# The adaLN product-sums of later stages issued from the scan's z units, and decayed x dt split one step later

## The chip, the cores and the metric

The kernel runs on one core of one Trainium2 chip. The metric is the device time of one execution in microseconds; the kernel before was run three times. Five engines work side by side: TensorE (PE; its weight loads are shown as PEld), VectorE (DVE), ScalarE (ACT), GpSimd (POOL) and SyncE (SP), which here issues nearly all DMAs. Each engine takes its instructions in the order in which the built program holds them; what they need from each other is settled by semaphores.

## What is computed

One block of a model with 512 tokens and a width of 1024, in float32. A vector c gives, through one 1024 x 6144 matrix, six vectors of 1024 that shift, scale and gate the two sub-layers:

```python
mod = (jax.nn.silu(c) @ w_ada[i] + b_ada[i])[:, None, :]
shift_m, scale_m, gate_m, shift_f, scale_f, gate_f = jnp.split(mod, N_MOD, axis=-1)
h = rmsnorm(x, norm_mix_w[i]) * (1.0 + scale_m) + shift_m
x = x + gate_m * hybrid_mixer(h, ...)
h = rmsnorm(x, norm_mlp_w[i]) * (1.0 + scale_f) + shift_f
x = x + gate_f * (jnp.square(jax.nn.relu(h @ w_up[i])) @ w_down[i])
```

The mixer projects h to z, x, B, C, dt, a pooling input and two gates. x, B and C pass a causal convolution of width 4 and a silu. Then a scan over 4 chunks of 128 tokens runs in 4 groups of 8 heads:

```python
scores = jnp.einsum('bclgn,bcsgn->bgcls', cc, bc)
mmat = scores[:, :, None] * segsum_decay(a_cs)
y_diag = jnp.einsum('bghcls,bcsghp->bclghp', mmat, x)
decay_states = jnp.exp(a_cs[..., -1:] - a_cs)
states = jnp.einsum('bcsgn,bghcs,bcsghp->bcghpn', bc, decay_states, x)
```

Here x is already multiplied by dt = softplus(dt_raw + bias). The scan's output is multiplied by silu(z) and normed by group; branch projections, sigmoid gates and an output projection follow, then the MLP.

## The kernel before

Every large product is made of *units*: 128 rows of an output, contracted over 1024. `unit` loads 512 KB of weights into a RAW slot (`load_unit`, L139; four slots d0 to d3), ACT rounds them to a high part (L144), DVE subtracts to get the low part (L145), both into one pair of the HL buffers, and PE makes 8 x 3 matmuls of 128x128 by 512 (L154 to L156: high x high, high x low, low x high). PSUM banks for units come from PU (three of them at this stage), those for the scan from PS.

A *product-sum* is `ada(j)` (L166 to L171): SP loads 512 KB of the transposed adaLN matrix into a RAW slot, the same four slots that the weights use, and one DVE instruction (L170) multiplies it by silu(c) and adds it up into one of 48 columns of `mod`; a second small one reads the accumulator. Sums 0 to 15 (shift and scale of the mixer) are made at the start, through other buffers. Sums 16 to 47 are needed from the output projection on: 16 to 23 gate the mixer, 24 to 39 shift and scale the MLP's input, 40 to 47 gate the MLP.

The stages follow each other so: the opening up to 53 us, where PE is fed h; a high-priority part (L329 to L364) that makes dt by a softplus chain of small DVE instructions (L340 to L354), sums it along tokens on PE (L356), copies the result (L357, which frees the PSUM bank), transposes it (L360) and writes it to DRAM (`cs_d`, `ecs_d`); the convolutions of group 0 (L381 to L383) and its four z units z0 to z3 (`u_z`); then `run`, which drives `ssd_group` for groups 0 to 3 and puts other units between its steps as fillers. z0 is given the PSUM bank that the softplus chain uses, so it cannot begin before L357.

In `ssd_group`, `prepare(c)` loads the decay rows of chunk c (L476), makes the decay factors (L478 to L480), masks (POOL, L481), exponentiates (L485), multiplies by the scores (L486), transposes x (L489), multiplies it by dt (L491), lets POOL multiply that by the decay (L497), and splits the product into a high part (ACT, L124) and a low part (DVE, L125). The main loop first prepares chunk c + 1 and then takes chunk c: it makes the state product with `mm3` (PE, L154 to L156 with two s tiles) and the output (L535).

The order on each engine is set when the program is built: a scheduler goes through the program by priority and by its own estimate of when each instruction could run. A moved call therefore moves other instructions too. Only the opening is written out by hand.

Of the kernel before, what the change touches and what calls it, by code (L numbers as in the profile page):

```python
# [61 lines left out]
def block_kernel(tc, xp, crow, arow, par, adaT, wstart, wz, wx, wpool_in, wgate, wpw, wbs, wbp, wout, wup, wdn, out):  # L62
# [3 lines left out]
    with (  # L66
# [13 lines left out]
        S = slots("s", NSLOT)  # L80
# [38 lines left out]
        done = [None]  # L119

        def split(src):

            hi, lo = S.get(F32R), S.get(F32R)
            act.copy(hi, src)  # L124
            done[0] = dve.tensor_tensor(lo, src, hi.bitcast(F32), ALU.subtract)  # L125
            return hi, lo
# [39 lines left out]
        def ada(j, at=RAW):  # L166

            r = at.get()
            sp.dma_start(r, adaT[j])
            dve.tensor_tensor_reduce(r, r, cbc, 1.0, col("b_ada", j), ALU.mult, ALU.add, mod[:, j:j + 1])  # L170
            at.put(r)  # L171

        def column_sums(ps, sqs, c0, c1, opened=False):

# [42 lines left out]
        with tc.manual_schedule():  # L217
# [74 lines left out]
            for k in range(8):  # L292
                hi, lo = S.get(F32R), S.get(F32R)
                h.append((hi, lo))
                t = S.get()
# [73 lines left out]
        for u in range(1, 7):  # L369
            t = S.get()  # L370
# [49 lines left out]
        def u_z(g, i):  # L420
            def f():
                if "sz" not in G[g]:
                    G[g]["sz"] = SZ.get()
                ps = unit(wz[4 * g + i], h)
                with tc.issue_after(act.activation(G[g]["sz"][:, i, :], ps, AF.Silu).ins):
                    silus()
                PU.put(ps)
            return f

        acc = [None] * 8  # L430

        def bs(g, jp):

            def f():
                w = load_unit(wbs[4 * g + jp])
                for jj in range(2):
                    j = 2 * jp + jj
                    ps = PU.get()
                    for k in range(4):
                        mm3(ps, w[4 * jj + k], G[g]["y"][k], k == 0, k == 3)  # L440
                    if g == 0:
                        acc[j] = S.get()
                        act.copy(acc[j], ps)
                    else:
                        dve.tensor_tensor(acc[j], acc[j], ps, ALU.add)
                    PU.put(ps)
                if jp == 3:
                    free(G[g]["y"])
            return f

        def ssd_group(g):
# [20 lines left out]
            def prepare(c):  # L472

                cc = slice(c * P, (c + 1) * P)
                m = MT.get()
                sp.dma_start(m, cs_d[heads, cc].partition_broadcast(P))  # L476
                if c < 3:
                    act.activation(cdg[:, c, :], m[:, :, P - 1], AF.Exp)  # L478
                    dve.tensor_tensor(decg[:, c, :], m[:, :, P - 1], ncs[:, c, heads], ALU.add)
                    act.activation(decg[:, c, :], decg[:, c, :], AF.Exp)  # L480
                pool.affine_select(  # L481
                    m, m, pattern=[[0, HG], [1, P]], compare_op=ALU.is_ge, fill=-1e30, base=0,
                    channel_multiplier=-1)
                for i in range(HG):
                    act.activation(m[:, i, :], m[:, i, :], AF.Exp, bias=ncs[:, c, g * HG + i:g * HG + i + 1])  # L485
                dve.tensor_tensor(m, m, sc[:, cc].unsqueeze(1).broadcast_to([P, HG, P]), ALU.mult)  # L486
                ps = PS.get()
                for i in range(4):
                    pe.transpose(ps[:, i * P:(i + 1) * P], xs[:, i, cc], ident)  # L489
                xdt = S.get()  # L490
                dve.tensor_tensor(  # L491
                    v3(xdt), v3(ps), dtk[:, c, heads].unsqueeze(2).broadcast_to([P, HG, 64]), ALU.mult)
                PS.put(ps)
                xd = None
                if c < 3:
                    t = S.get()
                    pool.tensor_tensor(  # L497
                        v3(t), v3(xdt), decg[:, c, :].unsqueeze(2).broadcast_to([P, HG, 64]), ALU.mult)
                    xd = split(t)
                    S.put(t)  # L500
                return m, xdt, xd

            ready = [prepare(0)]
            yield
            for c in range(NC):
                cc = slice(c * P, (c + 1) * P)
                if c < NC - 1:
                    ready.append(prepare(c + 1))
                    yield
                m, xdt, xd = ready.pop(0)  # L510
                yo = None
                if c > 0:
                    yo = PS.get()
# [112 lines left out]
        def pool_mix(gp):  # L626
            def f():
                w = load_unit(wpw[gp])
                for gi in (2 * gp, 2 * gp + 1):
                    for d in range(2):  # L630
                        ps = PU.get()
                        for k in range(2):
                            mm3(ps, w[((gi % 2) * 2 + d) * 2 + k], held[gi, k], k == 0, k == 1)
                        t = S.get()
                        act.activation(t, ps, AF.Copy, scale=col("pscale", 2 * gi + d))
                        PU.put(ps)
                        pout.append(split(t))
                        S.put(t)
                    free([held[gi, 0], held[gi, 1]])
            return f  # L640
# [45 lines left out]
        for j in range(8):  # L686
            gp = F.get()
            ps = unit(wgate[8 + j], h)
            behind(act.activation(gp, ps, AF.Sigmoid))
            PU.put(ps)  # L690
            merged.append(gp)
            if j == 1:
                for _ in rest:
                    pass
                later.append(SZ.get())
                F.free += range(12, 16)
                PU.free += PS.free
            if j == 3:
                for i in range(4):
                    bs(3, i)()  # L700
                pool_mix(1)()
            ada(16 + j)
        for j in range(8):
            ps = unit(wbp[j], pout)
            dve.tensor_tensor(merged[j], merged[j], ps, ALU.mult)
            PU.put(ps)
            ada(24 + j)
        free(pout)
        mg = []
        for j in range(8):  # L710
            gs = F.get()
            ps = unit(wgate[j], h)
            last = act.activation(gs, ps, AF.Sigmoid)
            PU.put(ps)
            dve.tensor_tensor(gs, gs, acc[j], ALU.mult)
            dve.tensor_tensor(gs, gs, merged[j], ALU.add)
            S.put(acc[j])
            F.put(merged[j])
            mg.append(split(gs))
            F.put(gs)  # L720
            with tc.issue_after(done[0].ins):
                ada(32 + j)
        free(h)
        with tc.issue_after(last.ins):
            table = act.preload_act_table_set("natural_log_exp_and_others")
# [42 lines left out]
        for j in range(5):  # L768
            ps = unit(wout[j], mg)
            residual(ps, j, 16)  # L770
            PU.put(ps)
            ada(40 + j)
            if j > 1:
                ada(43 + j)
        for k in range(8):
            dve.tensor_scalar(
                amod[:, 8 + k:9 + k], mod[:, 32 + k:33 + k], 1.0, col("nmlp", k), ALU.add, ALU.mult)
# [405 lines left out]
```

## Time and profile before

| what | us |
|---|---|
| runs of the kernel before, median of 3 | 968.84 |
| lowest, highest | 967.2, 969.86 |
| the profiled execution | 966.76 |
| its span, first to last instruction | 965.1 |

The profile comes from that one execution, so sums made from it are made against 966.76. In its rows a line number is one of the kernel before; names such as d, s, ps, xs and sz are tiles with their buffer numbers left out, d being weights, s work tiles and ps PSUM banks. A timeline row gives start, length, engine, line, operation, out<-in, shape and count, and in brackets the idle time of the engine ahead of it with what ended it.

### The profile page before, as it was taken

What the parts mean: (1) busy time and instruction counts of PE and PEld (TensorE: products, weight loads), DVE (VectorE), ACT (ScalarE), POOL (GpSimd) and SP (SyncE); (2) the same over time, 40 slices, a digit from 0 to 9 for tenths busy, and PEclk for the clock granted to TensorE, in tenths of its full rate; (3) what the DMA queues carried; (4) which work ended last, traced back from release to release, by engine and by line L of the source; (5) the groups of instructions that cost most, each with busy time, mean ns of one, the idle gap of its engine ahead of it and who ended that gap; (6) DMA issues with size and microseconds to landing.
All of it is one profiled execution on the core that took longest, in us unless ns stands there. A gap on an engine that the chain in (4) does not pass through costs nothing.

```text
span 965.1 us, 13244 instructions
## 1 busy us (share of the span) xinstructions
PE 948.7 (98%) x5131; PEld 803.7 (83%) x5131; DVE 657.5 (68%) x961; ACT 501.9 (52%) x814; POOL 88.5 (9%) x91
## 2 busy tenths in 40 slices
PE   7999999999999999999999999999999999999996
PEld 4778887888888888888888878998899889889986
DVE  7995958467866787978533888895557556665533
ACT  6488887667528542563312334684257127415632
POOL 0103211220312132300000000000000000000000
PEclk9999999999999999999999999999999999999998
DMA  9747423433253334437632678442143224204002
GB/s 370 274 138 206 128 92 120 131 110 109 78 155 115 99 102 131 131 100 254 213 101 96 206 258 269 140 142 75 46 144 131 66 77 164 88 33 154 22 1 88
DMA packets 61761, 129.22 MB, mean 134 GB/s; under 512 B 4673, under 2 KB 29377, under 8 KB 61698
## 3 DMA queue, kind: packets, MB, share of 16 engines
q1 hardware_dynamic: 61696, 128.38, 41.1%
q8 instruction: 40, 0.66, 0.3%
q14 instruction: 23, 0.19, 0.1%
q10 hardware_dynamic: 2, 0.00, 0.0%
HBM read 126.13 MB, written 2.23 MB: 133 GB/s over the span
## 4 chain that ended last, share of the span: by engine, by line
PE 88%; DVE 5%; ACT 3%; DMA 2%; issue 1%; POOL 0%; SPq 0%; DVEq 0%; ACTq 0%; POOLq 0%
PE ps L154 23%; PE ps L155 23%; PE ps L156 22%; PE ps L881 12%; PE ps L315 3%; PE ps L535 2%; PE ps L515 1%; DVE d L170 1%; DMA d<-adaT 1%; DMA d<-xp 1%; PE ps L489 1%; ACT d L144 1%; DMA d<-wout 1%; DVE d L145 0%; DMA d<-wup 0%
## 5 line engine op out<-in xcount | busy, mean ns | idle before, releaser
L154 PE MATMUL ps<-s,d 128*128 128x512 f32 (+1 forms) x1088 | 415.3, 382 | 3.4 <-DVE s L383 1.4
L155 PE MATMUL ps<-s,d 128*128 128x512 f32 (+1 forms) x1088 | 411.2, 378 | 0.0
L156 PE MATMUL ps<-s,d 128*128 128x512 f32 (+1 forms) x1088 | 411.0, 378 | 0.0
L154 PEld LDWEIGHTS ps<-s,d 128*128 128x128 f32 x1088 | 204.1, 188 | 45.2 <-issue 3.6
L156 PEld LDWEIGHTS ps<-s,d 128*128 128x128 f32 x1088 | 204.2, 188 | 38.7 <-DVE d L145 0.3
L155 PEld LDWEIGHTS ps<-s,d 128*128 128x128 f32 x1088 | 204.3, 188 | 37.5 <-DVE s L125 0.2
L145 DVE TENSOR_TENSOR d<-d,d 128x1024 fp32r<-128x1024 f32 x89 | 111.9, 1259 | 68.9 <-ACT d L144 67.8
L144 ACT CAST d<-d 128x1024 fp32r<-128x1024 f32 x89 | 93.0, 1046 | 124.8 <-PE ps L155 114.9
L881 PE MATMUL ps<-s,d 128*128 128x256 f32 x864 | 103.8, 279 | 0.0
L881 PEld LDWEIGHTS ps<-s,d 128*128 128x128 f32 x864 | 102.9, 188 | 0.2
L822 ACT CAST d<-d 128x1024 fp32r<-128x1024 f32 x44 | 45.8, 1050 | 79.1 <-PE ps L155 62.8
L822 ACT CAST d<-sz 128x1024 fp32r<-128x1024 f32 x32 | 33.7, 1052 | 68.8 <-PE ps L155 48.9
L1070 DVE SCALAR_TENSOR_TENSOR xs<-ps,mod,xs 128x512 f32<-128x512 f32 x29 | 21.8, 750 | 69.7 <-PE ps L156 69.7
L823 DVE TENSOR_TENSOR d<-d,d 128x1024 fp32r<-128x1024 f32 x44 | 53.5, 1224 | 21.9 <-ACT d L822 20.3
L823 DVE TENSOR_TENSOR d<-sz,d 128x1024 fp32r<-128x1024 f32 x32 | 39.2, 1224 | 19.7 <-ACT d L822 18.3
L170 DVE CUSTOM_DVE_ANT_0 d<-d,d,par_t 128x1024 f32<-128x1024 f32 x32 | 41.7, 1306 | 8.6 <-DMA d<-adaT 8.5
L485 ACT ACTIVATE d<-d,ncs 128x128 f32<-128x128 f32 x128 | 40.3, 391 | 6.2 <-POOL d L481 6.1
L383 DVE SCALAR_TENSOR_TENSOR s<-ps,par_t,s 128x511 f32<-128x511 f32 (+2 forms) x54 | 39.8, 742 | 0.3
L315 PE MATMUL ps<-s,d 128*128 128x512 f32 x144 | 35.2, 396 | 2.2 <-ACT s L303 2.2
L315 PEld LDWEIGHTS ps<-s,d 128*128 128x128 f32 x144 | 26.3, 188 | 10.1 <-ACT s L303 4.8
L125 DVE TENSOR_TENSOR s<-s,s 128x512 fp32r<-128x512 f32 x32 | 26.9, 843 | 4.7 <-ACT s L124 4.6
L124 ACT CAST s<-s 128x512 fp32r<-128x512 f32 x32 | 19.7, 619 | 19.5 <-POOL s L497 16.0
(215 smaller groups left out, 999.8 us busy)
## 6 DMA issues: line engine op xcount, KB each, us to landing
d<-adaT SPq DMA_DIRECT2D x32, 512.0 KB, 4.2
d<-wx SPq DMA_DIRECT2D x18, 512.0 KB, 3.6
d<-wdn SPq DMA_DIRECT2D x18, 512.0 KB, 3.7
d<-wz SPq DMA_DIRECT2D x16, 512.0 KB, 3.9
d<-cs_d SPq DMA_DIRECT2D x16, 512.0 KB, 5.9
d<-wbs SPq DMA_DIRECT2D x16, 512.0 KB, 3.5
d<-wgate SPq DMA_DIRECT2D x16, 512.0 KB, 3.5
sz<-wdn SPq DMA_DIRECT2D x14, 512.0 KB, 4.1
```

The costliest lines, as they stand in the source:

```text
L144: act.copy(hi[:, :w], r[:, a:a + w])
L145: (low or dve).tensor_tensor(lo[:, :w], r[:, a:a + w], hi[:, :w].bitcast(F32), ALU.subtract)
L154: pe.matmul(ps, whi, xhi[:, t0:t1], start=start, stop=False)
L155: pe.matmul(ps, whi, xlo[:, t0:t1], start=False, stop=False)
L156: pe.matmul(ps, wlo, xhi[:, t0:t1], start=False, stop=stop)
L170: dve.tensor_tensor_reduce(r, r, cbc, 1.0, col("b_ada", j), ALU.mult, ALU.add, mod[:, j:j + 1])
L315: pe.matmul(first[u], w[u][i // 2], h[k][i % 2], start=k == 0 and i == 0, stop=k == 7 and i == 2)
L383: dve.scalar_tensor_tensor(t[:, sh:], ps[:, :T - sh], w(3 - sh), t[:, sh:], ALU.mult, ALU.add)
L485: act.activation(m[:, i, :], m[:, i, :], AF.Exp, bias=ncs[:, c, g * HG + i:g * HG + i + 1])
L822: act.copy(dst[0], src)
L823: dve.tensor_tensor(dst[1], src, dst[0].bitcast(F32), ALU.subtract)
L881: pe.matmul(ps, x, y, start=start and m == 0 and i == 0, stop=m == 3 and i == 2, skip_group_check=True)
```

## The change

A list of the sums 16 to 47 is made, and `ada_next` takes the next one from it. It is called after each z unit (four of group 0, then one in each z unit among the fillers of groups 0 to 2), after each of the first eight gate units and each of the four `bs(3, i)`, and after the first four `wbp` units: 16 + 8 + 4 + 4 = 32. The calls at the old places (gate units, `wbp` units, second gate units, output units) are gone. And in `ssd_group` the split of decayed x dt moves from `prepare(c)` to the beginning of the loop's step c, ahead of the preparation of chunk c + 1.

```diff
+        rows = list(range(16, 48))
+
+        def ada_next(n=1):
+
+            for _ in range(n):
+                ada(rows.pop(0))
...
             PU.put(ps)
+                ada_next()
             return f
...
-                    xd = split(t)
-                    S.put(t)
+                    xd = t
                 return m, xdt, xd
...
                 cc = slice(c * P, (c + 1) * P)
+                m, xdt, xd = ready.pop(0)
                 if c < NC - 1:
+                    t, xd = xd, split(xd)
+                    S.put(t)
                     ready.append(prepare(c + 1))
                     yield
-                m, xdt, xd = ready.pop(0)
...
+            ada_next()
             if j == 3:
                 for i in range(4):
                     bs(3, i)()
+                    ada_next()
                 pool_mix(1)()
-            ada(16 + j)
...
             PU.put(ps)
-            ada(24 + j)
+            if rows:
+                ada_next()
...
-            with tc.issue_after(done[0].ins):
-                ada(32 + j)
...
-            ada(40 + j)
-            if j > 1:
-                ada(43 + j)
```

In the changed kernel the lines stand lower: L340 to L364 are L347 to L371, L383 is L390, L460 is L468, L468 is L476, L479 is L487, L489 is L497, L491 is L499. What the scheduler makes of it is shown at three places, as rows of the two built programs. In them L170 ISA is a product-sum (and, as a second row, the reading of its accumulator).

First PE, from the end of the unit that runs ahead of the cumulative sum to the beginning of z0 (ps_109 in both). Before, ps_113 (z1) and ps_117 (z2) are both done there, and ps_152 is a unit of group 1:

```order
L156 MATMUL ps_117_640<-s_76_435,d_116_637 128x512
L460 MATMUL ps_124_700<-ident,s_97_535 128x128 x3
L468 MATMUL ps_125_706<-s_99_542,s_97_535 128x128
L356 MATMUL ps_89_484<-s_88_482,tri 128x128
L468 MATMUL ps_125_706<-s_99_542,s_97_535 128x128 x3
L489 MATMUL ps_128_729<-ident,xs_100_544 128x128
L489 MATMUL ps_134_759<-ident,xs_100_544 128x128
L154 MATMUL ps_152_839<-s_34_174,d_150_835 128x512
L155 MATMUL ps_152_839<-s_35_175,d_150_835 128x512
L156 MATMUL ps_152_839<-s_34_174,d_151_836 128x512
L360 MATMUL ps_27_167<-ident,ncs 32x128 x4
L154 MATMUL ps_109_576<-s_34_174,d_107_572 128x512
```

The same place in the changed program, where ps_114 is z1 and ps_119 is z2; the row that follows is z0's first matmul:

```order
L156 MATMUL ps_114_611<-s_76_435,d_113_608 128x512
L468 MATMUL ps_128_712<-ident,s_97_535 128x128 x3
L476 MATMUL ps_129_718<-s_99_542,s_97_535 128x128 x2
L154 MATMUL ps_119_646<-s_34_174,d_117_642 128x512
L155 MATMUL ps_119_646<-s_35_175,d_117_642 128x512
L476 MATMUL ps_129_718<-s_99_542,s_97_535 128x128 x2
L497 MATMUL ps_132_741<-ident,xs_100_544 128x128
L497 MATMUL ps_138_771<-ident,xs_100_544 128x128
L497 MATMUL ps_132_741<-ident,xs_100_544 128x128
L497 MATMUL ps_138_771<-ident,xs_100_544 128x128
L363 MATMUL ps_89_484<-s_88_482,tri 128x128
L367 MATMUL ps_27_167<-ident,ncs 32x128 x4
```

One unit less is done ahead of these steps, and of z2 two matmuls are. The other 22 of z2 now come behind z0.

Second DVE, at the beginning of the softplus chain. Before:

```order
L145 TENSOR_TENSOR d_108_573<-d_106_570,d_107_572 128x1024
L145 TENSOR_TENSOR d_112_605<-d_110_602,d_111_604 128x1024
L145 TENSOR_TENSOR d_116_637<-d_114_634,d_115_636 128x1024
L340 COPY dtk<-ps_89_484 128x128
L341 TENSOR_TENSOR dtk<-dtk,ps_89_484 128x128
L342 SCALAR_TENSOR_TENSOR s_85_479<-dtk 128x128
L352 TENSOR_SCALAR dtk<-dtk 128x128
L344 TENSOR_SCALAR s_86_480<-s_85_479 128x128
```

The same place in the changed program, from the first product-sum on (z0's subtraction stands ahead of it, as above):

```order
L170 ISA d_110_602,mod<-d_110_602,d_5_82,par_t 128x1024
L170 ISA mod 128x1
L145 TENSOR_TENSOR d_113_608<-d_111_605,d_112_607 128x1024
L170 ISA d_115_637,mod<-d_115_637,d_5_82,par_t 128x1024
L170 ISA mod 128x1
L347 COPY dtk<-ps_89_484 128x128
L348 TENSOR_TENSOR dtk<-dtk,ps_89_484 128x128
L349 SCALAR_TENSOR_TENSOR s_85_479<-dtk 128x128
L359 TENSOR_SCALAR dtk<-dtk 128x128
L170 ISA d_120_672,mod<-d_120_672,d_5_82,par_t 128x1024
L170 ISA mod 128x1
L351 TENSOR_SCALAR s_86_480<-s_85_479 128x128
```

Two product-sums came ahead of the chain and one into it, in front of L351 (L344 before); z2's subtraction went behind the chain. Between L351 and the chain's last step L361 the changed program holds thirteen convolution steps (L390) and one subtraction, the program before nine and one.

Third DVE, where group 0's scan begins (dec is the decay factor, L479 or L487; the target of L491 or L499 is x dt; L486 or L494 multiplies by the scores). Before:

```order
L479 TENSOR_TENSOR dec_80<-d_127_712,ncs 128x8
L491 TENSOR_TENSOR s_129_734<-ps_128_729,dtk 128x512
L491 TENSOR_TENSOR s_135_764<-ps_134_759,dtk 128x512
L479 TENSOR_TENSOR dec_80<-d_133_742,ncs 128x8
L486 TENSOR_TENSOR d_127_712<-d_127_712,ps_125_706 128x1024
L125 TENSOR_TENSOR s_132_739<-s_130_736,s_131_738 128x512
```

The changed program:

```order
L145 TENSOR_TENSOR d_143_783<-d_141_780,d_142_782 128x1024
L487 TENSOR_TENSOR dec_80<-d_131_724,ncs 128x8
L145 TENSOR_TENSOR d_166_914<-d_164_911,d_165_913 128x1024
L487 TENSOR_TENSOR dec_80<-d_137_754,ncs 128x8
L487 TENSOR_TENSOR dec_80<-d_159_884,ncs 128x8
L499 TENSOR_TENSOR s_133_746<-ps_132_741,dtk 128x512
```

All three decay rows, each of which waits for its load, now stand ahead of the first x dt; before, x dt of two chunks came right behind the first. On SP, between the first and the second of these loads, the changed program issues one weight load (into the slot d1 that the first row above frees).

## The prediction

> **What bounds the kernel now.** I read the page first, then TensorE's waits, then a table by stretches, then the timeline of each engine where the change moves something.
>
> ```profile
> span 965.1 us, 13244 instructions
> PE 948.7 (98%) x5131; PEld 803.7 (83%) x5131; DVE 657.5 (68%) x961; ACT 501.9 (52%) x814; POOL 88.5 (9%) x91
> PE 88%; DVE 5%; ACT 3%; DMA 2%; issue 1%; POOL 0%; SPq 0%; DVEq 0%; ACTq 0%; POOLq 0%
> ```
>
> PE is busy nearly all of the span and carries 88% of the chain that ended last. So an edit on DVE can gain only what PE waits for today, while it can lose as much as it makes PE wait. Between the opening and the end PE waits in few places:
>
> ```profile
> PE ps L154 <- DVE s L383: 1.4, 1, 1.4
> PE ps L154 <- ACT s L124: 1.0, 1, 1.0
> PE ps L154 <- ACT d L144: 0.5, 1, 0.5
> ```
>
> The first lies at 166 us (boundary of scan groups 0 and 1), the others at 573 and 587 us (last gate and first output units). Together 2.9 us: that is about all that can be won. The stretches say where DVE has room for a product-sum (the columns after the length are PE, PEld, DVE, ACT, POOL busy):
>
> ```profile
> 58.00:68.00 10.00, 9.95 (x53) 8.12 (x52) 10.00 (x21) 8.53 (x13) 0.00 (x0) 1.00 0.20 56
> 90.00:130.00 40.00, 40.00 (x225) 32.91 (x225) 35.77 (x59) 34.01 (x71) 12.67 (x13) 1.00 0.46 140
> 210.00:300.00 90.00, 90.00 (x465) 74.24 (x465) 63.59 (x93) 51.09 (x91) 17.58 (x18) 1.00 0.40 114
> 480.00:520.00 40.00, 40.00 (x178) 33.10 (x178) 13.97 (x15) 8.93 (x9) 0.00 (x0) 1.00 0.30 93
> ```
>
> From 210 us on there is room; from 58 to 68 us DVE has no idle time at all, and three of the moved sums now stand just ahead of that.
>
> **Term 1, the first z units: +9.2 us.** Here PE runs two whole units (z1, z2) while DVE works off the softplus chain; only then come the cumulative sum (L356), its transposes (L360) and z0, which needs the chain's PSUM bank:
>
> ```profile
> 53.42 0.50 PE L154 MATMUL ps<-s,d 128*128 128x512 f32 x1 [0.44 <-ACT s L373]
> ...
> 64.22 0.39 PE L156 MATMUL ps<-s,d 128*128 128x512 f32 x1
> 64.45 0.49 PE L460 MATMUL ps<-ident,s 128*128 128x128 f32 x3
> ...
> 65.06 0.49 PE L356 MATMUL ps<-s,tri 128*128 128x128 f32 x2
> ...
> 67.34 0.60 PE L360 MATMUL ps<-ident,ncs 128*32 128x128 f32 x4
> 67.69 0.48 PE L154 MATMUL ps<-s,d 128*128 128x512 f32 x1
> ```
>
> 48 matmuls start from 53.42 to 64.22, 0.23 us apart. When z0 begins, 24 + 24 + 3 = 51 unit matmuls are done. In the changed program only z1 and two matmuls of z2 stand ahead of z0: 26. The 25 others come to 25 x 0.23 = 5.7 us of cover, and they are now queued behind L363 and L367, the same two steps. Does the chain end earlier to make up for it? Its rows on DVE:
>
> ```profile
> 48.19 2.37 DVE L145 TENSOR_TENSOR d<-d,d 128x1024 fp32r<-128x1024 f32 x2
> 51.21 1.23 DVE L145 TENSOR_TENSOR d<-d,d 128x1024 fp32r<-128x1024 f32 x1 [0.65 <-PE ps L309]
> 52.35 0.29 DVE L340 COPY dtk<-ps 128x128 f32<-128x128 f32 x1
> ...
> 53.33 0.23 DVE L352 TENSOR_SCALAR dtk<-dtk 128x128 f32<-128x128 f32 x1
> 54.10 0.23 DVE L344 TENSOR_SCALAR s<-s 128x128 f32<-128x128 f32 x1 [0.55 <-ACT s L343]
> ...
> 55.89 0.74 DVE L383 SCALAR_TENSOR_TENSOR s<-s,par_t,s 128x511 f32<-128x511 f32 x1
> 56.55 0.22 DVE L348 TENSOR_SCALAR s<-s 128x128 f32<-128x128 f32 x1
> ...
> 64.72 0.28 DVE L354 TENSOR_TENSOR s<-dtk,ea 128x128 f32<-128x128 f32 x1
> ```
>
> and a product-sum with its load:
>
> ```profile
> L170 DVE CUSTOM_DVE_ANT_0 d<-d,d,par_t 128x1024 f32<-128x1024 f32 x32 | 41.7, 1306 | 8.6 <-DMA d<-adaT 8.5
> ...
> d<-adaT SPq DMA_DIRECT2D x32, 512.0 KB, 4.2
> ```
>
> A weight subtraction takes 1.14 us start to start (51.21 to 52.35), a product-sum some 1.25. From 48.19 DVE now does z0's subtraction, a sum, z1's subtraction, a sum: 48.19 + 2 x 1.14 + 2 x 1.25 = 53.0, where the four short steps begin (before 52.35). They take 1.2 us (52.35 to 53.56) and end at 54.2. Then comes the third sum, and this is the new wait: its load takes the RAW slot that the first sum frees at 48.19 + 1.14 + 1.25 = 50.6, and lands 4.2 us later, at 54.8; the sum ends near 56.2. Behind it on DVE stands the whole chain from L351 (before L344, at 54.10), behind that PE's L363, L367 and z0. From 54.10 to the end of L354, 65.00, are 10.9 us with nine convolution steps (0.66 each, 55.89 to 56.55) and one subtraction; the new order has thirteen and one, 4 x 0.66 = 2.6 more. So the chain ends at 56.2 + 10.9 + 2.6 = 69.7, and with L363, L364, L367 (0.49, 0.28, 0.60) z0 begins at about 71.2 instead of 67.7. PE's delay: 3.5 + 5.7 = 9.2 us. Were the third load always early, the sum would end at 55.5: 8.5. If the new steps on DVE cost nothing, the lost cover alone is 5.7. If the loads land 2 us later, 11.2. I take 9.2, which each of its rows gives.
>
> **Term 2, the first state product: +2 us.** It needs decayed x dt, and that needs the decay rows, whose loads are queued on SP:
>
> ```profile
> 70.91 1.02 SPq L476 DMA_DIRECT2D d<-cs_d  x2
> ...
> 76.96 0.22 ACT L478 ACTIVATE cd<-d 128x8 f32<-128x8 f32 x1 [0.35 <-DMA d<-cs_d]
> ...
> 80.56 0.22 ACT L478 ACTIVATE cd<-d 128x8 f32<-128x8 f32 x1 [3.19 <-DMA d<-cs_d]
> ```
>
> Before, the first two loads are issued together and land after 6.0 and 9.2 us, and DVE scales x by dt right after the first one. Now the three decay sums stand ahead of that on DVE, so it waits for the third load; and SP issues the second and third only after a weight load for whose slot a cast must run, which needs z0's buffer: z0 ends at 71.2 + 5.5 = 76.7, cast and subtraction 1.05 + 1.14, so issue at about 79.5 and landing 6 to 12 us later, 85.5 to 91.5.
>
> ```profile
> 78.31 1.05 POOL L497 TENSOR_TENSOR s<-s,dec 128x512 f32<-128x512 f32 x1
> ...
> 83.22 0.60 ACT L124 CAST s<-s 128x512 fp32r<-128x512 f32 x1
> ...
> 86.08 0.39 PE L154 MATMUL ps<-s,s 128*128 128x512 f32 x1
> ```
>
> Behind the landing come dt scaling, POOL's product (1.05) and ACT's cast, which began 4.9 us after POOL's start: some 6 us in all, so the product could start at 91.5 to 97.5. PE itself gets there at 71.2 + 4 x 5.5 = 93.2. The wait is 0 to 4.3; I take 2.
>
> **Term 3, what is won: -1.4 us.**
>
> ```profile
> 565.61 1.28 DVE L170 CUSTOM_DVE_ANT_0 d<-d,d,par_t 128x1024 f32<-128x1024 f32 x1 [0.80 <-DMA d<-adaT]
> ...
> 573.21 0.74 PE L154 MATMUL ps<-s,d 128*128 128x512 f32 x2 [0.97 <-ACT s L124]
> ...
> 586.95 0.50 PE L154 MATMUL ps<-s,d 128*128 128x512 f32 x1 [0.46 <-ACT d L144]
> ```
>
> The sums at 550 to 592 us, with their loads, held up DVE's products of the gates and wout's loads. They are gone from there, and nothing takes their place: 0.97 + 0.46. The stretch rows above hide the sums of the later z units (63.59 of 90 us on DVE) and of the gate units (13.97 of 40).
>
> **Term 4, the rest: 0.** The split one step later adds no instruction; in the built order of group 1 the run of three score products ahead of the convolution that ends the 1.4 us wait at 166 us is still there, and ACT's cast still waits for POOL there. Gain between 0 and 1.4; I take 0. The sums in group 0's scan add 4 x 1.25 = 5 us to a DVE with 40.00 - 35.77 = 4.2 idle: 0 to 4; I take 0, since PE shows no wait in that row.
>
> **Sum:** 9.2 + 2 - 1.4 = +9.8 us on the profiled execution's 966.76 (span 965.1 and 1.66 around it): 976.6. The median of the three runs, 968.84, is 2.1 above that execution; the forecast for it is 968.84 + 9.8 = 978.6.
>
> **Rivals.** (a) PE's clock drops in the new gap. The end of the trace shows that it can:
>
> ```profile
> 958.00:960.00 2.00, 0.00 (x0) 0.00 (x0) 1.14 (x2) 0.79 (x2) 0.00 (x0) 0.96 0.00 0
> 960.00:965.10 5.10, 0.00 (x0) 0.00 (x0) 1.34 (x3) 0.00 (x0) 0.00 (x0) 0.50 0.61 206
> ...
> 1.25 4.16 PE L212 MATMUL ps<-s 128*128 128x512 bf16 x12 [1.25 <-DVE s L199]
> ...
> 11.53 1.24 PE L212 MATMUL ps<-s 128*128 128x512 bf16 x5
> ```
>
> Two microseconds after the last matmul the granted clock is 0.50. Between z1's end (53.42 + 5.5 = 58.9) and z0 PE has 12.3 us with some 2.5 us of work. The price of a cold start: the first twelve warming matmuls took 4.16, later ones 1.24 for five, so 4.16 - 12 x 0.248 = 1.2 us. Term 2's wait would hide part of it. With all of it: 979.8, chance 0.15. [...]
>
> (b) DVE becomes the bound in group 0's scan. For it: 35.77 of 40 us busy and 5 us more. Against it: PE waits nowhere in that row. At its upper end of 4 us: 982.6, chance 0.12.
>
> (c) Not slower: the softplus chain is ready when z1 ends. Then PE's reordering costs nothing, only the gains stay: 968.84 - 1.4 = 967.4, with the wait at 166 us gone as well 966.0. It decides where z0 starts by 67.7 - 5.7 + 2 = 64.0 us; the chain would have to end near 62.5, and against that stands DVE's full row from 58 to 68. Chance 0.18, of which 0.05 below 965.9.
>
> **How the numbers follow.** Forecast 0.55, (a) 0.15, (b) 0.12, (c) 0.18. About 0.3% (2.9 us) is what a measurement of this kernel can tell from no change: faster is below 965.9, slower above 971.7. Slower 0.55 + 0.15 + 0.12 = 0.82, same 0.13, faster 0.05. With term 1 at 5.7, term 2 at 0 and both gains the forecast is 971.7; with 11.2, 4.3 and 1.4 it is 982.9. For 8 in 10 the range goes on to 985 for (b), and down to 969.5 for a part of (c).
>
> **What would show it.** Term 1: a PE wait of several us behind z1, and z0's first matmul near 71 us, 26 unit matmuls after 53.4; a DVE wait for adaT of about half a microsecond near 54 us. Term 2: the first state product at 93 to 98 us, released by ACT's cast. Term 3: no PE wait at 570 to 590 us. Rival (a): a granted clock under 1.00 between 60 and 80 us. If z0 starts before 66 us, term 1 is wrong and with it the sign.

## The result, and the profile after

The changed kernel takes 977.72 us (median of five runs, 977.12 to 978.21), the kernel before 968.06 us in the same comparison (median of five, 967.2 to 969.86): ratio 1.0101, 95% interval 1.009 to 1.0113, or 9.7 us slower. The forecast was +9.8. The profiled execution took 978.08 us with a span of 976.4, which is 11.3 us above the profiled execution of before; 0.95 of that lies in the opening, which the change does not touch and which differs by up to 2 us between the executions below. In what follows, "shifted" times are moved so that the first z unit's first matmul stands at 53.42 us in every kernel (for the changed kernel: minus 0.95).

The page of the changed kernel, its first lines, the row of granted clock in 40 slices, and the shares of the chain that ended last:

```profile
span 976.4 us, 13242 instructions
PE 953.7 (98%) x5131; PEld 805.9 (83%) x5131; DVE 654.7 (67%) x961; ACT 499.1 (51%) x812; POOL 92.1 (9%) x91
PEclk9989999999999999999999999999999999999998
PE 81%; DVE 10%; DMA 3%; ACT 2%; issue 2%; POOL 1%; SPq 0%; DVEq 0%; ACTq 0%; POOLq 0%
```

TensorE's share of the chain fell from 88% to 81%, DVE's rose from 5% to 10%: a piece of the path has moved to DVE, and the third slice of the clock (49 to 73 us) shows an 8. The table by stretches says where (length; PE, PEld, DVE, ACT and POOL busy; clock; DMA share; GB/s):

```profile
60.00:65.00 5.00, 1.49 (x8) 1.35 (x7) 5.00 (x11) 4.97 (x8) 0.00 (x0) 0.84 0.10 39
65.00:70.00 5.00, 2.50 (x10) 1.88 (x9) 5.00 (x13) 2.37 (x5) 0.00 (x0) 0.82 0.34 108
70.00:75.00 5.00, 4.32 (x17) 3.32 (x18) 4.77 (x9) 2.32 (x4) 0.00 (x0) 0.66 0.05 13
...
90.00:130.00 40.00, 38.92 (x212) 30.97 (x211) 35.76 (x54) 34.80 (x62) 10.59 (x12) 1.00 0.52 159
575.00:605.00 30.00, 30.00 (x132) 24.42 (x131) 17.86 (x24) 14.83 (x21) 0.00 (x0) 1.00 0.39 125
605.00:625.00 20.00, 20.00 (x152) 19.21 (x151) 11.50 (x23) 6.95 (x14) 0.00 (x0) 1.00 0.24 79
```

From 60 to 70 us PE works 4 of 10 us while DVE has no idle time; at 575 to 625 us it no longer waits. PE's timeline between z1 and the first state product:

```profile
54.37 0.50 PE L154 MATMUL ps<-s,d 128*128 128x512 f32 x1 [0.44 <-ACT s L380]
...
59.73 0.39 PE L156 MATMUL ps<-s,d 128*128 128x512 f32 x1
63.63 0.90 PE L468 MATMUL ps<-ident,s 128*128 128x128 f32 x3 [3.52 <-ACT s L405]
...
65.08 0.80 PE L154 MATMUL ps<-s,d 128*128 128x512 f32 x1
65.68 0.63 PE L155 MATMUL ps<-s,d 128*128 128x512 f32 x1
...
67.71 0.44 PE L497 MATMUL ps<-ident,xs 128*128 128x128 f32 x2 [0.65 <-ACT xs L405]
70.30 0.69 PE L497 MATMUL ps<-ident,xs 128*128 128x128 f32 x2 [2.15 <-ACT xs L405]
70.78 0.66 PE L363 MATMUL ps<-s,tri 128*128 128x128 f32 x2
71.82 1.03 PE L367 MATMUL ps<-ident,ncs 128*32 128x128 f32 x4 [0.39 <-DVE ncs L364]
72.51 0.78 PE L154 MATMUL ps<-s,d 128*128 128x512 f32 x1
...
73.81 0.40 PE L154 MATMUL ps<-s,d 128*128 128x512 f32 x1
...
96.21 0.50 PE L154 MATMUL ps<-s,s 128*128 128x512 f32 x1 [1.08 <-ACT s L124]
```

z1 ends, PE stands 3.52 us, does two matmuls of z2, stands again, and z0 begins at 72.51, when 26 unit matmuls are done. The silus (L405) that end these waits hang on DVE's convolutions. DVE in the same stretch:

```profile
56.30 1.28 DVE L170 CUSTOM_DVE_ANT_0 d<-d,d,par_t 128x1024 f32<-128x1024 f32 x1 [1.25 <-DMA d<-adaT]
...
57.51 0.22 DVE L351 TENSOR_SCALAR s<-s 128x128 f32<-128x128 f32 x1
...
70.30 0.28 DVE L361 TENSOR_TENSOR s<-dtk,ea 128x128 f32<-128x128 f32 x1
...
88.63 0.17 DVE L487 TENSOR_TENSOR dec<-d,ncs 128x8 f32<-128x8 f32 x1 [2.20 <-DMA d<-cs_d]
90.16 0.17 DVE L487 TENSOR_TENSOR dec<-d,ncs 128x8 f32<-128x8 f32 x1 [1.36 <-DMA d<-cs_d]
90.25 0.68 DVE L499 TENSOR_TENSOR s<-ps,dtk 128x512 f32<-128x512 f32 x1
```

The third sum waits 1.25 us for its load, ahead of the chain from L351; and x times dt (L499) stands behind the third decay row.

A ledger of the two profiled executions: at equal matmul work (a matmul of 512 columns counted as 0.2266 us, since the starts of unit matmuls mostly lie 0.226 or 0.227 us apart in both traces, smaller ones in proportion) PE in the changed kernel is later by so much:

| stretch, in times of before | lag at its end | change |
|---|---|---|
| opening, up to 53 us | 0.95 | +0.95 |
| z units to just behind the first state product, 53 to 100 us | 12.46 | +11.5 |
| end of group 0, 135 us | 13.56 | +1.1 |
| the wait at 166 us, gone | 11.94 | -1.6 |
| 397 and 435 us, two new waits | 13.56 | +1.6 |
| 572 to 607 us, three waits gone | 11.34 | -2.2 |
| rest | 11.34 | 0 |

The new small waits, at the end of group 0, at the first pooling mix and in a branch projection of group 3:

```profile
146.36 0.50 PE L581 MATMUL ps<-s,ones 128*128 128x512 f32 x1 [0.46 <-ACT s L124]
...
409.57 0.50 PE L154 MATMUL ps<-s,d 128*128 128x512 f32 x1 [0.64 <-ACT s L644]
...
447.00 0.50 PE L155 MATMUL ps<-s,d 128*128 128x512 f32 x1 [0.22 <-DVE s L125]
```

So nearly all of the loss lies between 53 and 100 us, and the rest cancels to about -1.

### The profile page after: what moved, and what is told of

It is laid out like the page before. It is cut to its first block, busy times and chain, and to the rows that moved or that the text cites. A ratio compares the mean times of both kernels' runs of the same rounds, so it can differ in the third digit from the quotient of the medians.

```text
span 976.4 us, 13242 instructions
## 1 busy us (share of the span) xinstructions
PE 953.7 (98%) x5131; PEld 805.9 (83%) x5131; DVE 654.7 (67%) x961; ACT 499.1 (51%) x812; POOL 92.1 (9%) x91
## 4 chain that ended last, share of the span: by engine, by line
PE 81%; DVE 10%; DMA 3%; ACT 2%; issue 2%; POOL 1%; SPq 0%; DVEq 0%; ACTq 0%; POOLq 0%
PE ps L154 22%; PE ps L155 22%; PE ps L156 22%; PE ps L887 12%; PE ps L544 1%; DVE d L145 1%; DVE s L125 1%; DVE d L170 1%; PE ps L524 1%; DVE pad L626 1%; DMA d<-adaT 1%; DMA d<-cs_d 1%; DVE s L390 1%; PE ps L497 1%; DMA sz<-adaT 1%
## 5 line engine op out<-in xcount | busy, mean ns | idle before, releaser
L154 PE MATMUL ps<-s,d 128*128 128x512 f32 (+1 forms) x1088 | 416.0, 383 | 1.2 <-ACT s L644 0.6
L156 PE MATMUL ps<-s,d 128*128 128x512 f32 (+1 forms) x1088 | 411.3, 378 | 0.0
L154 PEld LDWEIGHTS ps<-s,d 128*128 128x128 f32 x1088 | 204.5, 188 | 42.6 <-issue 2.2
L156 PEld LDWEIGHTS ps<-s,d 128*128 128x128 f32 x1088 | 204.3, 188 | 38.7 <-issue 0.2
L170 DVE CUSTOM_DVE_ANT_0 d<-d,d,par_t 128x1024 f32<-128x1024 f32 x32 | 42.6, 1331 | 11.3 <-DMA d<-adaT 11.2
L390 DVE SCALAR_TENSOR_TENSOR s<-ps,par_t,s 128x511 f32<-128x511 f32 (+2 forms) x54 | 40.0, 741 | 0.2
L124 ACT CAST s<-s 128x512 fp32r<-128x512 f32 x32 | 19.7, 620 | 35.4 <-POOL s L505 23.1
L125 DVE TENSOR_TENSOR s<-s,s 128x512 fp32r<-128x512 f32 x32 | 24.3, 766 | 7.9 <-ACT s L124 7.9
```

The source lines that it names most:

```text
L154: pe.matmul(ps, whi, xhi[:, t0:t1], start=start, stop=False)
L156: pe.matmul(ps, wlo, xhi[:, t0:t1], start=False, stop=stop)
L390: dve.scalar_tensor_tensor(t[:, sh:], ps[:, :T - sh], w(3 - sh), t[:, sh:], ALU.mult, ALU.add)
```

## The experiments

Each ratio is to runs of the kernel before on the same chip in the same comparison. "Lag" is that of the ledger, without the opening's part. One table first, since most readings rest on it; times are shifted, and the lag is that at 110 us of before. In most kernels it has about that value soon behind the first state product; in e3 and e11 it is still 0 there, and what the table shows for them comes between 97 and 110 us:

| kernel | unit matmuls ahead of z0 | z0 starts | first state product | lag | ratio |
|---|---|---|---|---|---|
| before | 51 | 67.69 | 86.07 | 0 | 1 |
| changed | 26 | 71.56 | 95.25 | 11.5 | 1.0101 |
| e1_not_in_group0 | 51 | 67.68 | 86.01 | 0 | 1.0014 |
| e2_only_group0 | 26 | 70.65 | 93.91 | 10.1 | 1.0122 |
| e3_split_alone | 51 | 67.68 | 86.01 | 1.3 | 0.9993 |
| e4_split_as_before | 26 | 70.34 | 93.79 | 10.1 | 1.0136 |
| e6_loads_alone | 26 | 66.52 | 92.46 | 10.2 | 1.0098 |
| e7_products_alone | 72 | 73.19 | 94.37 | 3.2 | 1.0028 |
| e9_other_buffers | 26 | 68.88 | 93.77 | 9.5 | 1.0084 |
| e11_sums_after_z3 | 60 | 69.53 | 87.38 | 3.6 | 1.0054 |
| e14_bank_last | 50 | 70.57 (z2) | 93.77 | 7.2 | 1.0076 |

### Which part costs: four kernels

**e1_not_in_group0**, from the changed kernel:

```diff
-                ada_next()
+                if g:
+                    ada_next()
```

> The changed kernel without the four product-sums in group 0's z units (four more follow in the second half of the wbp units; the split stays one step late). TensorE's built order is the old one again there: z1 and z2, 48 unit matmuls, ahead of the cumulative sum. Theory (terms 1 and 2 lie in these four sums): the 11 us between 53 and 97 us go, the gains at 570 to 610 us stay, so about 967 us, ratio to the kernel before 0.997 to 1.000, z0's first matmul near 68 us, no TensorE wait over 1 us at 58 to 100 us. Rival (the other 28 sums in the scan, or the split, cost it): 972 us or more, ratio 1.004 or more.

Measured: 968.75 us against 967.92, ratio 1.0014 (1.0002 to 1.0026). The 11 us are gone and z0 is back at 67.68. The ratio lies just above the range given: the waits at 572 to 607 us are gone (-2.2), but those at 397 and 435 us are there (+1.75 by the ledger) and the one at 166 us has grown from 1.6 to 2.4.

**e2_only_group0**, from the kernel before:

```diff
                 PU.put(ps)
+                if g == 0:
+                    ada(16 + i)
...
-            ada(16 + j)
+            if j > 3:
+                ada(16 + j)
```

> The kernel before, with sums 16 to 19 taken from the first four gate units and put into group 0's four z units; nothing else of the change. Theory: terms 1 and 2 alone, +11 us (9.2 + 2, and nothing won at 573 and 587 us): about 979 us, ratio 1.010 to 1.013, a TensorE wait of 3 to 4 us behind z1. Rival (the sums of the later stages or the split cost it): within 2 us of the kernel before, ratio 0.998 to 1.002.

Measured: 978.88 us against 967.92, ratio 1.0122 (1.0108 to 1.0135). Four sums out of 32, moved alone, cost as much as the whole change; the gap behind z1 is the same:

```profile
64.20 0.90 PE L462 MATMUL ps<-ident,s 128*128 128x128 f32 x3 [3.52 <-ACT s L398]
```

**e3_split_alone**, the kernel before with the change's two places in `ssd_group` and nothing else:

```diff
-                    xd = split(t)
-                    S.put(t)
+                    xd = t
...
+                m, xdt, xd = ready.pop(0)
                 if c < NC - 1:
+                    t, xd = xd, split(xd)
+                    S.put(t)
...
-                m, xdt, xd = ready.pop(0)
```

> The kernel before, with the split of decayed x dt one step later and no other edit. Theory (term 4: it adds no instruction): 0, or up to 1.6 us faster if it is what takes the wait at 166 us away: 966.5 to 968.5 us, ratio 0.998 to 1.0005. Rival (the later split holds up the state products): 970 us or more, ratio above 1.002, with new waits of TensorE for ACT's cast in the scan.

Measured: 967.01 us against 967.92, ratio 0.9993 (0.9984 to 1.0002): no difference that can be told. The wait at 166 us is gone here, but PE arrives there 1.7 us later, from two new waits for the split (1.3 at 99 us, 0.4 at 135 us, start to start): nothing is won up to there.

**e4_split_as_before**, the changed kernel with that diff reversed.

> The changed kernel with the split of decayed x dt put back at the end of each preparation; the sums stay where the change put them. Theory (the split is worth 0 to 1.6 us, the sums all the rest): 977.5 to 979.5 us, ratio 1.0095 to 1.012; if the wait at 166 us is back here, the split had taken it away. Rival (the split is the cost): 970 us or less, ratio below 1.003.

Measured: 980.11 us against 967.92, ratio 1.0136 (1.0121 to 1.0152), 0.0035 or 3.4 us above the changed kernel, whose interval lies wholly below. Two waits stand in its trace that the changed kernel does not have, at 302 and 333 us:

```profile
301.90 1.16 PE L523 MATMUL ps<-s,s 128*128 128x128 f32 x8 [1.15 <-DVE s L535]
...
333.06 0.47 PE L154 MATMUL ps<-s,d 128*128 128x512 f32 x1 [1.04 <-DVE s L390]
```

Start to start they cost 1.3 and 1.2 us. So the later split is worth nothing alone, and about 2.5 us where sums crowd DVE in the scan. The wait at 166 us is gone in this kernel too, without the later split, and it stays in e1 with it: it depends on the order that the scheduler builds, and no single edit here decides it.

### What it is in four sums: loads, DVE's time, or the slots

**e6_loads_alone**, from the kernel before:

```diff
                 PU.put(ps)
+                if g == 0:
+                    r = RAW.get()
+                    sp.dma_start(r, adaT[16 + i])
+                    RAW.put(r)
```

> The kernel before, with four extra loads of adaT rows into RAW slots, one behind each of group 0's z units; nothing reads them, DVE gets no instruction more. TensorE's built order is that of the changed kernel (26 unit matmuls ahead of the cumulative sum), DVE's chain is that of before. Theory (the loads alone push z2's weights back, and with them 25 unit matmuls of cover): z0 near 68 us with 26 units done, so 5.7 us lost, and 0 to 4.3 at the first state product: 973.5 to 978 us, ratio 1.006 to 1.0105. Rival (DVE's time for the sums is the cost): within 2 us of before, ratio 0.998 to 1.002.

**e7_products_alone**, from the kernel before (the result is overwritten by the real sum later):

```diff
                 PU.put(ps)
+                if g == 0:
+                    m = MT.get()
+                    dve.tensor_tensor_reduce(
+                        m.rearrange("p h k -> p (h k)"), cbc, cbc, 1.0, col("b_ada", 16 + i), ALU.mult, ALU.add, mod[:, 16 + i:17 + i])
+                    MT.put(m)
```

> The kernel before, with four extra product-sums in group 0's z units that read resident data: the same DVE instruction, no load and no RAW slot. DVE's chain gets the sums ahead of it, as in the changed kernel; TensorE's built order keeps z1, z2 and puts a unit of group 1 ahead of the cumulative sum. Theory (it is the cover that is lost, not DVE's time): the chain ends 4 to 6 us later behind 5.4 us of other units, 0 to +2: 967.5 to 970.5 us, ratio 0.9995 to 1.0025. Rival (DVE's time for the sums is the cost): 974 us or more, ratio 1.006 or more.

**e9_other_buffers**, from the changed kernel: group 0's four sums use the scan's `MT` buffers.

```diff
+        def ada_mt():
+            j, m = rows.pop(0), MT.get()
+            r = m.rearrange("p h k -> p (h k)")
+            sp.dma_start(r, adaT[j])
...
+            MT.put(m)
...
-                ada_next()
+                if g:
+                    ada_next()
+                else:
+                    ada_mt()
```

> The changed kernel, with group 0's four sums loaded into the three buffers that the scan's decay rows use later instead of RAW slots; each sum still has its load, behind its z unit. TensorE's built order stays that of the changed kernel (26 unit matmuls ahead of the cumulative sum). Theory (the 512 KB transfers push z2's weights back, whatever slot they land in): still slow, ratio to the kernel before 1.007 to 1.012, 974.5 to 979.5 us. Rival (the sums' holding of RAW slots is what costs): 971 us or less, ratio 1.003 or less.

Measured: loads alone 978.29 us against 967.86, ratio 1.0098 (1.0077 to 1.0118); products alone 970.97 against 967.86, 1.0028 (1.0014 to 1.0041); other buffers 975.86 against 967.30, 1.0084 (1.0066 to 1.0102). Four loads that nobody reads cost what the change costs. The same four DVE instructions without loads leave a lag of 3.2 us behind the first state product, although z0 starts later than anywhere else (73.19): 72 unit matmuls are done by then. Their total lies just above the range given; one more wait is in it, at the norm of the output stage, in a kernel that has 36 later sums. The clock stands at 0.50 behind it, from 611.38 to 614.80:

```profile
611.24 1.11 PE L767 MATMUL ps<-sz,ones 128*128 128x256 f32 x2 [2.45 <-DVE sz L758]
```

And RAW slots are not what costs: without them most of it stays. What remains is that transfers of 512 KB stand ahead of z2's weights in the queue, and that the built order then puts z2's matmuls behind z0. Whether the weights would have come too late for the old order on PE, no run shows.

But e6 also shows something that the forecast had not: without the sums on DVE the chain is early and z0 starts at 66.52, so by the forecast's own working PE should be late by 25 x 0.227 - 1.2 = 4.5 us; and by the ledger it is, 3.9 to 4.9 us, until the first state product. Rows of e6, PE first, then DVE, then ACT, then the stretch behind the wait:

```profile
67.30 0.48 PE L154 MATMUL ps<-s,d 128*128 128x512 f32 x1
...
93.24 0.50 PE L154 MATMUL ps<-s,s 128*128 128x512 f32 x1 [3.54 <-ACT s L124]
```

```profile
84.91 0.17 DVE L483 TENSOR_TENSOR dec<-d,ncs 128x8 f32<-128x8 f32 x1 [0.96 <-DMA d<-cs_d]
...
86.72 0.68 DVE L495 TENSOR_TENSOR s<-ps,dtk 128x512 f32<-128x512 f32 x1
```

```profile
92.59 0.60 ACT L124 CAST s<-s 128x512 fp32r<-128x512 f32 x1
```

```profile
93.64:97.06 3.42, 3.42 (x18) 2.01 (x17) 2.19 (x3) 3.42 (x10) 0.00 (x0) 0.50 0.14 35
```

There PE waits 3.54 us: x times dt (L495) stands behind the third decay row's step on DVE, and the cast (L124) ends 6.5 us after that began. The lag becomes 10.2, the same as in e2, which has the sums on DVE and z0 4.1 us later. Not all of that is the wait: PE was busy for 0.40 of the 3.41 us ahead of 93.64, and then the clock is at 0.50 for 3.41 us. From the state product's first matmul to the start of the last of the sixteen small ones behind it are 4.0 us here and 2.7 in the changed kernel, which runs at 1.00 there and has one unit matmul more in between; so an estimated 1.5 of the 10.2 (4.0 - 2.7 + 0.23) are the clock's, and that the lag is just that of e2 is chance. The runs fit: three with a mean clock of 0.992 or 0.993 took 978.2 to 978.6 us, the one with 0.996 took 975.9. **Two limits lie one behind the other**: PE's lost cover, and a first state product that cannot begin before 92.5 to 95 us.

### Can the cover be had back: three kernels

**e11_sums_after_z3**, from the changed kernel:

```diff
-                ada_next()
+                if g:
+                    ada_next()
+                elif i == 3:
+                    ada_next(4)
```

> The changed kernel, with group 0's four sums called together behind its last z unit instead of one behind each; everything else of the change stays. Their loads then follow the four weight loads, and TensorE's built order has z1, z2 and 12 matmuls of a group 1 unit ahead of z0. Theory (what costs is that loads of sums stand ahead of z2's weights): 966 to 970 us, ratio 0.998 to 1.002, no TensorE wait over 1.5 us at 58 to 75 us. Rival (four sums anywhere ahead of the scan cost it, by DVE's time or the loads' bandwidth): 974 us or more, ratio 1.006 or more.

Measured: 973.6 us against 967.86, ratio 1.0054 (1.004 to 1.0068), between the two. The theory holds up to 95 us: no lag, first state product at 87.38. Then the four late loads and sums cost elsewhere, which the theory had not counted: the low half of the split waits on DVE, and a unit waits for ACT's copy of a branch projection (the starts before are 99.20 and 174.43). Behind the first the clock is at 0.50 for 3.41 us, from 102.74; behind the second the matmuls that start from 178.10 to 178.96 are 0.43 us apart instead of 0.23. Both are part of the price:

```profile
101.47 0.50 PE L155 MATMUL ps<-s,s 128*128 128x512 f32 x1 [1.79 <-DVE s L125]
...
176.71 0.50 PE L154 MATMUL ps<-s,d 128*128 128x512 f32 x1 [1.89 <-ACT s L454]
```

**e14_bank_last**, from the changed kernel:

```diff
-        PU.put(tk)
...
-        PU.put(*first[8 - NPU:])
+        PU.put(*first[8 - NPU:], tk)
```

> The changed kernel, with the softplus chain's PSUM bank put back behind the two free ones, so that z0 and z1 need no bank of the chain and z2 gets it: TensorE's built order has z0, z1 and two matmuls of z3, 50 unit matmuls, ahead of the cumulative sum. All sums stay. Theory A (lost cover is the larger part of term 1 and comes back in the time): 5.4 us less than the changed kernel, 971 to 973 us, ratio 1.003 to 1.0055. Theory B (the first state product, which needs the chain's end and then the decay rows, cannot begin much before 94 us whatever TensorE does until then): the cover is regained up to 90 us and lost again in a wait of 4 to 6 us for the first state product: 975.5 to 978 us, ratio 1.0075 to 1.0105. No clock below 1.00 between 60 and 75 us under either, if rival (a) of the forecast came from the gap.

Measured: 975.04 us against 967.30, ratio 1.0076 (1.0061 to 1.0092). 24 more unit matmuls (5.4 us) stand ahead of the chain's steps on PE, and the ratio falls by 0.0025, 2.4 us (the two intervals just touch). The result lies between theory A and theory B, at B's edge: ahead of the state product the lag is 5.0 to 5.8 us where the changed kernel has 9.3 to 10.1, with a new wait of 1.89 us for z2's low half in it, and behind it 7.2. The first state product still starts at 93.77, as in e2, e4 and e9. The last sentence of the expectation fell: the clock is at 0.50 from 69.28 to 72.69 us. Rows of PE and of ACT:

```profile
74.25 0.50 PE L156 MATMUL ps<-s,d 128*128 128x512 f32 x1 [1.89 <-DVE d L145]
...
93.71 0.60 ACT L124 CAST s<-s 128x512 fp32r<-128x512 f32 x1
```

Here it is not x times dt that comes late: it stands ahead of the second decay row (85.91), and POOL's product of it ends at an estimated 87.7, since in e6 it ends 1.8 us after x times dt began (86.72 to 88.53). The cast still begins only at 93.71, some 6 us later, and ACT has no idle time in between: it does two table loads of 1.28 us each, a silu, a weight cast and exponentials first. So in this kernel ACT's order sets the limit; in e6 the same stretch, from 88.53 to 92.59, is 4.1 us.

**e15_filled_gap**, from the changed kernel (`last_mm[0]` is z1's last matmul):

```diff
             u_z(0, i)()
+            if i == 1:
+                ps = PS.get()
+                with tc.issue_after(last_mm[0].ins), tc.high_priority():
+                    for _ in range(12):
+                        pe.matmul(ps, ones_r, h[0][0], start=True, stop=True)
+                PS.put(ps)
```

> The changed kernel, with twelve extra matmuls (ones by h, into a free PSUM bank; nothing reads the result) behind z1's last one, 2.7 us of TensorE work in its 3.5 us gap; the order of everything else on TensorE is kept. Theory (rival (a) of the forecast has come about, the clock is at 0.50 in two stretches between 63 and 74 us, and it is a small part of the cost): the granted clock stays 1.00 from 55 to 75 us, z0's first three matmuls start 0.23 us apart instead of 0.3 to 0.6, and 0.5 to 1.2 us come back: ratio 1.0085 to 1.010. Rival (the clock is the larger part): 973 us or less, ratio 1.006 or less. If the fillers only hold up the steps behind them: ratio 1.0105 or more.

Measured: 977.92 us against 967.58, ratio 1.0104 (1.0089 to 1.0119): nothing won. With the fillers the clock was at 1.00 up to 69.29 us, and then at 0.50 for 6.8 us instead of two times 3.4, just when z0 runs (L156 to L158 of this kernel are L154 to L156 of the others):

```profile
72.35 0.78 PE L156 MATMUL ps<-s,d 128*128 128x512 f32 x1
72.93 0.63 PE L157 MATMUL ps<-s,d 128*128 128x512 f32 x1
73.35 0.63 PE L158 MATMUL ps<-s,d 128*128 128x512 f32 x1
...
75.49 0.63 PE L157 MATMUL ps<-s,d 128*128 128x512 f32 x1
```

Nine matmuls of z0 start 0.43 us apart instead of 0.23. So the drop cost an estimated 9 x 0.20 = 1.8 us here. In the changed kernel only z0's first three or so fall into it.

### Two versions that might have beaten both

**e8_late_rows**, from e3 (`ada_next` takes from 32 to 47):

```diff
                 PU.put(ps)
+                if g:
+                    ada_next()
...
                     bs(3, i)()
+                    ada_next()
...
-            with tc.issue_after(done[0].ins):
-                ada(32 + j)
...
-            ada(40 + j)
-            if j > 1:
-                ada(43 + j)
```

> A version that might beat both: the kernel before with the later split, and only sums 32 to 47 (those of the second gate units and of the output units) moved, 12 to the z units of groups 1 to 3 and 4 behind the bs units of group 3; group 0's z units get none and sums 16 to 31 stay. Theory (the waits at 572, 586 and 607 us come from sums 32 to 47): those three waits, 2.2 us, are gone, the wait at 166 us as with the split alone: 964.5 to 967 us, ratio 0.9965 to 0.999. Rival (every sum in the scan costs about as much as it wins): 967.5 us or more, ratio 0.9995 or more.

Measured: 970.15 us against 967.86, ratio 1.0022 (1.0013 to 1.0031): slightly slower. The three waits are gone (-2.2), but 2.5 us stand at 168 us where e3 has none, and 1.9 at 435 us (start to start). The rival's reading holds: what the sums win late they cost in the scan.

**e16_one_stage_ahead**, from e3:

```diff
             ada(24 + j)
+            ada(32 + j)
...
-            with tc.issue_after(done[0].ins):
-                ada(32 + j)
```

> A version that might beat both: the kernel before with the later split, and only sums 32 to 39 moved, one stage ahead, from the second gate units to the wbp units; no sum goes into the scan. Theory (the wait at 572 us comes from these sums on DVE, and DVE has room in the wbp units): that wait, 1.1 us, is gone, the rest as with the split alone: 965 to 967 us, ratio 0.997 to 0.9995. Rival (it only moves the wait): 967 to 968.5 us, ratio 0.9995 to 1.001.

Measured: 966.39 us against 967.58, ratio 0.9989 (0.9977 to 1.0): the lowest ratio of all, and yet not told from no change. The wait at 572 us, which the theory meant to remove, is still there (1.15 start to start); those at 586 and 607 us, 0.6 and 0.5 before and 0.2 each in e3, are gone.

## Why the prediction came out right, step by step

**Term 1 (+9.2).** Its rows came as worked out. 26 unit matmuls stand ahead of z0. The third sum's wait for its load was larger (1.25 us for about half a microsecond); L351 began at 56.56 shifted (the sum was to end at 56.2), the chain ended at 69.63 (69.7), z0 began at 71.56 (71.2). PE's delay by the same rule is 3.87 + 25 x 0.227 = 9.55. That the lost cover comes with the loads is shown by e6 (loads alone, 26 ahead) and e11 (loads behind the weights, 60 ahead). The later start of z0 is DVE's time for the sums: without them z0 starts at 66.52 (e6). Up to the first state product that is about half of the lag (3.9 to 4.9 in e6, 9.3 to 10.1 in the changed kernel); in the total it hardly shows, since the second limit stands behind it.

**Term 2 (+2).** The state product came at 95.25 shifted, inside 91.5 to 97.5, released by ACT's cast after a wait of 1.08; the lag rose from 9.55 to 11.5, by 2. What the prediction did not say is that this term is not a small addition but a second limit at nearly the same place. Had term 1 been nothing, term 2 would not have stayed at 2: e6 has 4 to 5 us before it and loses the rest there, an estimated 1.5 of it to the clock; e14 regains 5.4 us of cover and keeps 2.4 of it. By this reading rival (c), too, was mispriced: a chain that is ready when z1 ends would not have made the kernel as fast as before unless the decayed x times dt and its cast came as early. Which of DVE's, SP's and ACT's order sets that second limit was read from rows, not tried apart by an edit; the rows differ, with x times dt late in e6 and the cast late in e14. The 2 us themselves were picked from a range of 0 to 4.3, and that they came out so well is in part luck.

**Term 3 (-1.4).** Right in kind and too small: 2.2 were won. The idle times 0.97 and 0.46 are 1.13 and 0.62 from start to start, and a third wait, at 607 us (0.46 start to start), was not counted.

**Term 4 (0).** The step that was off. The wait at 166 us went (-1.6) where the prediction left it, and three new ones came: one at the end of group 0 (+1.1), inside the 0 to 4 that was kept for that scan, and two at 397 and 435 us (+0.9, +0.7), which the prediction did not have at all. In sum +1.1. "The split adds no instruction" is true, but it is worth about 2.5 us beside the sums (e4) and nothing alone (e3).

The sum, 11.2 for terms 1 and 2, measured 11.5; terms 3 and 4, -1.4, measured -1.1. The latter is luck: 0.8 us more were won and 1.1 us more lost than forecast, two misses that nearly cancel. That the medians differ by 9.7 and not by 10.4 is within the runs' scatter.

**Rivals.** (a) came about, and was small: the clock was 0.50 in two stretches, and z0's first three matmuls took 1.3 us (72.51 to 73.81) instead of 0.7. The two steps ahead of z0, L363 and L367, took 0.66 and 1.03 us instead of 0.49 and 0.60. Part of the rest fell into waits, so the forecast was not far off without a term for it. The 1.2 us that (a) adds came from the first matmuls of the trace of before, where the profile gives the clock as 1.00 (0 to 6 us): that a lower clock made them long was the author's estimate. The clock fell in other runs too: in e6, e7 and e11 single waits on PE, of 3.54, 2.45 and 1.79 us, were followed by 3.41 us at 0.50, which in e6 cost an estimated 1.5 us. (b) did not: DVE is busy 35.76 of 40 us at 90 to 130 us, as before, and PE's missing 1.08 us there is the wait of term 2. The 1.1 us at the end of group 0 lie behind that stretch, and what they come from was not tried. (c) did not: z0 started at 71.56, far from 64.

## What to carry to other kernels

Work that is moved into "free" time of one engine brings its loads with it; here the loads, queued ahead of weights that cover a serial chain, cost 1% (e6) while the moved arithmetic by itself cost 0.3% (e7). Ask of each load that is put into a queue what stands behind it, and what that was hiding. And when a wait is removed, look for the next limit close behind it before its whole length is booked as a gain.

## What the hardware showed beyond that

For a lower clock rival (a) had only the 0.50 behind the last matmul of before to go by. In the runs the clock was at 0.50 also in stretches in which PE works. Rows of the changed kernel, then of e14_bank_last, then of e15_filled_gap, cut where the clock changes and elsewhere to the same length (columns as above):

```profile
60.00:63.41 3.41, 0.12 (x1) 0.00 (x0) 3.41 (x10) 3.38 (x5) 0.00 (x0) 1.00 0.14 56
63.41:66.83 3.42, 3.20 (x13) 2.99 (x13) 3.42 (x7) 2.94 (x5) 0.00 (x0) 0.50 0.17 29
66.83:70.24 3.41, 0.67 (x4) 0.24 (x3) 3.41 (x9) 1.25 (x2) 0.00 (x0) 1.00 0.33 130
70.24:73.65 3.41, 2.96 (x11) 2.23 (x12) 3.18 (x7) 0.74 (x3) 0.00 (x0) 0.50 0.00 0
```

```profile
65.86:69.28 3.42, 1.24 (x12) 1.00 (x10) 3.18 (x7) 1.72 (x5) 0.00 (x0) 1.00 0.24 75
69.28:72.69 3.41, 3.07 (x10) 1.77 (x10) 3.19 (x6) 1.61 (x3) 0.00 (x0) 0.50 0.20 78
72.69:76.10 3.41, 1.85 (x8) 1.54 (x9) 3.41 (x5) 3.37 (x5) 0.00 (x0) 1.00 0.32 69
```

```profile
62.47:65.88 3.41, 2.39 (x14) 1.54 (x13) 3.41 (x7) 3.41 (x6) 0.00 (x0) 1.00 0.00 0
65.88:69.29 3.41, 0.33 (x1) 0.14 (x1) 3.41 (x10) 0.87 (x2) 0.00 (x0) 1.00 0.47 154
69.29:72.71 3.42, 2.19 (x8) 1.54 (x9) 3.19 (x8) 0.63 (x1) 0.00 (x0) 0.50 0.00 0
72.71:76.12 3.41, 3.41 (x9) 2.64 (x9) 3.41 (x5) 3.34 (x4) 0.00 (x0) 0.50 0.36 77
```

In these rows the clock was at 0.50 for 3.41 us at a time, and in e15 for 6.83. Of the 3.41 us ahead of a drop PE was busy for 0.12, 0.67, 1.24 or 0.33; behind a stretch with 2.39 us busy the clock was still 1.00. Behind stretches at 0.50 with 3.20, 2.96, 3.07 or 3.41 us busy it was 1.00 again (in the changed kernel from 73.65 us, in e15 from 76.12), behind one with 2.19 it was still 0.50. So PE was not wholly idle ahead of these drops, and in e11_sums_after_z3 it was busy for 1.62 us (99.33 to 102.74) ahead of one. The busy time alone does not tell them: after 1.54 us in the opening of the changed kernel (12.21 to 15.63) the clock stayed at 1.00. What decides, no run shows.
